# Forming two Strassen weight sums with a plain transfer and an adding transfer instead of a VectorE addition

## The chip, the cores and the metric

The kernel runs on one core of one Trainium2 chip. The metric is the device time of one execution in microseconds; lower is better. Engines are named as in the profile: PE is TensorE, DVE is VectorE, ACT is ScalarE, POOL is GpSimd and SP is SyncE. SP computes nothing here and issues all transfers of the kernel before. POOL does a few small operations.

## The reference

One decoder block in float32 on 512 tokens of width 1024: a half feed-forward layer with layer norm, a mixer (retention beside a convolution) with layer norm, and a second half feed-forward layer with layer norm.

```
def swiglu_ffn(h, w_gate, w_up, w_down):
    return (jax.nn.silu(h @ w_gate) * (h @ w_up)) @ w_down

x = layer_norm(alpha * x + 0.5 * swiglu_ffn(x, ffn1_w_gate, ffn1_w_up, ffn1_w_down), ln1_g, ln1_b)
m = hybrid_mixer(x, w_in, ...)
x = layer_norm(alpha * x + m, ln2_g, ln2_b)
x = layer_norm(alpha * x + 0.5 * swiglu_ffn(x, ffn2_w_gate, ffn2_w_up, ffn2_w_down), ln3_g, ln3_b)
```

The width of the feed-forward layers is 2816, which is 22 blocks of 128 columns. The change touches only the products with `w_gate` and `w_up`.

## The kernel before

**Precision.** Each float32 operand is split into a high part, which ACT makes by rounding to fp32r, and a low part, which DVE makes by subtracting the high part. Each product is three matmuls: high by high, high by low, low by high.

**Strassen units.** A feed-forward layer loads one unit of 128 x 2048 numbers (1 MB) for each of the 22 column blocks: gate and up weights together. The first units are done in the ordinary way (2 in the first layer, 3 in the second), the other 20 and 19, 39 in all, by a seven-product form of Strassen's method (Winograd's). For it the unit counts as four blocks of 128 x 512, in memory in the order a22, a12, a11, a21 (`raw[:, 0]` to `raw[:, 3]`). The weights that the products need are a12 and a11 as they are; s1 = a22 + a21 and s3 = a11 + a21; s2 = s1 + a11 and s4 = s2 + a12; and a22 as it is.

**Steps of one unit** (`strassen_w`, from line 144). `load` (L161) brings the unit into `raw`, on SP. `s13` (L165) forms s1 and s3 in one DVE addition into a tile `st`. `s24` (L169, L170) forms s2 and s4 from them and `raw`, in another `st` tile. `hi_a`, `hi_b`, `hi_c`, `hi_d` are the high parts on ACT (L155): of `raw` for a12 and a11, of the first `st` for s1 and s3, of the second `st` for s2 and s4 (named `chi`), of `raw` for a22 (`dhi`). `lo_a` to `lo_d` are the low parts on DVE (L158).

**Order.** The code around it is under a manual schedule: each engine does its instructions in the order in which they are written. In turn u of the loop in `strassen_rows` (from line 183), TensorE multiplies unit u (all at L201, 84 matmuls), while ACT and DVE prepare unit u + 1. A turn ends on DVE with `row2` (L226), which takes differences of PSUM banks; the second of them, `row2(prev, 1)`, stands at the head of the next turn and must be done before TensorE adds the s4 product into the same bank. Before the loop, the first unit is prepared among the steps that form the x operands (`f1` to `f4` at L125 and L127, `th` and `tl` at L135 and L138). These use the `st` tiles too.

**Buffers.** `raw` has two buffers, so the load of unit u + 2 waits for `lo_d` of unit u. `st` has three, taken in turn. In the first layer the order is f3, f1, s13 of the first unit, f2, s24 of the first unit, f4, s13 of the second unit: the last takes the buffer of f2 and so waits for f4, which reads f2. In the second layer s13 of the second unit takes the buffer of f1, whose last reader is `lo1` (the second of the two L138 instructions in a row).

Of the kernel before, what the change touches and what calls it, by code (L numbers as in the profile page):

```python
# [8 lines left out]
F32 = mybir.dt.float32  # L9
F32R = mybir.dt.float32r  # L10
AF = mybir.ActivationFunctionType
ALU = mybir.AluOpType
# [3 lines left out]
P = 128  # L16
# [36 lines left out]
def block_kernel(ctx, tc, ap, out):  # L53
    nc = tc.nc
# [92 lines left out]
    def strassen_w(pool, src):  # L147

        raw = wpool.tile([P, 4, 512], F32, name="raw", tag="raw", bufs=2)
        w, s = {}, {}  # L150

        def parts(n, shape, src, names, tag="w"):
            hi = (wpool if tag == "w" else pool).tile(shape, F32R, name=tag + "hi", tag=tag + "hi", bufs=n)
            lo = (wpool if tag == "w" else pool).tile(shape, F32R, name=tag + "lo", tag=tag + "lo", bufs=n)
            nc.scalar.copy(hi, src)  # L155
            for i, name in enumerate(names):
                w[name] = hi[:, i], lo[:, i]
            return lambda: nc.vector.tensor_tensor(lo, src, hi.bitcast(F32), op=ALU.subtract)  # L158

        def load():  # L160
            nc.sync.dma_start(raw, src.rearrange("p (b c) -> p b c", b=4))  # L161

        def s13():
            s[13] = pool.tile([P, 2, 512], F32, name="st", bufs=3)
            nc.vector.tensor_tensor(s[13], raw[:, 0:4:2], raw[:, 3:4].to_broadcast([P, 2, 512]), op=ALU.add)  # L165

        def s24():
            s[24] = pool.tile([P, 2, 512], F32, name="st", bufs=3)
            nc.vector.tensor_tensor(s[24][:, 0], s[13][:, 0], raw[:, 2], op=ALU.add)  # L169
            nc.vector.tensor_tensor(s[24][:, 1], s[24][:, 0], raw[:, 1], op=ALU.add)  # L170

        lo = {}

        def hi_a():
            lo["a"] = parts(4, [P, 2, 512], raw[:, 1:3], ("a12", "a11"))

        def hi_b():
            lo["b"] = parts(4, [P, 2, 512], s[13], ("s1", "s3"))

        def hi_c():  # L180
            lo["c"] = parts(2, [P, 2, 512], s[24], ("s2", "s4"), "c")

        def hi_d():
            lo["d"] = parts(2, [P, 1, 512], raw[:, 0:1], ("a22",), "d")

        return dict(w=w, load=load, s13=s13, s24=s24, hi_a=hi_a, hi_b=hi_b, hi_c=hi_c, hi_d=hi_d,
                    lo_a=lambda: lo["a"](), lo_b=lambda: lo["b"](), lo_c=lambda: lo["c"](), lo_d=lambda: lo["d"]())

# [450 lines left out]
    with ExitStack() as mix:  # L639
# [25 lines left out]
        with tc.tile_pool(name="heads", bufs=1) as hp_:  # L665
# [137 lines left out]
            for hp in range(H // 2):  # L803
                a, b = 2 * hp, 2 * hp + 1
# [199 lines left out]
```

## Time and profile before

| What | Value |
|---|---|
| Time, median of 3 runs (lowest, highest) | 1391.82 us (1391.26, 1392.65) |
| Time of the profiled execution | 1392.91 us |
| Its span, first to last instruction | 1391.1 us |
| Granted TensorE clock over the span | 0.996 |
| PE busy | 1373.3 us, 99% |
| DVE busy | 996.0 us, 72% |
| ACT busy | 597.5 us, 43% |
| POOL busy | 21.8 us, 2% |
| Transfers | 150.83 MB, 108 GB/s over the span |

The span is the time between the first and the last instruction on the core. The 1.8 us by which the profiled execution is longer lie around it. A share in the table is an average over stages: the Strassen stages run from about 30 to 238 us and from about 1067 to 1263 us of the span.

### The profile page before, as it was taken

How to read it: one execution, taken by the hardware profiler on the slowest of the kernel's cores; microseconds unless marked ns; L12 is line 12 of the kernel's file. 1: busy time of each engine (PE TensorE's matmuls, PEld its weight loads, DVE VectorE, ACT ScalarE, POOL GpSimd, SP SyncE). 2: the span in 40 equal slices, each digit the busy share in tenths (PEclk: the TensorE clock that was granted, in tenths of full speed). 3: DMA queues.
4: the chain of work that ended last, by engine and by line, in shares of the span. 5: the costliest groups of instructions: out<-in, count | busy, mean ns of one | idle time of the engine just before them, and what ended most of it. 6: DMA issues, size and time to landing. Idle time of an engine off the chain costs nothing.

```text
span 1391.1 us, 19272 instructions
## 1 busy us (share of the span) xinstructions
PE 1373.3 (99%) x7974; PEld 1218.3 (88%) x7974; DVE 996.0 (72%) x1422; ACT 597.5 (43%) x872; POOL 21.8 (2%) x36
## 2 busy tenths in 40 slices
PE   9899999999999999999999999999999999999997
PEld 7899999888988888888888888888889999998886
DVE  7888886434787787786787997555488887874336
ACT  5555555323434433434345522382333554544221
POOL 0000000000000000000000000000000000000000
PEclk9999999999999999999999999999999999999999
DMA  5323232524422222222221233232250323225221
GB/s 187 122 91 122 92 119 96 210 92 148 155 76 72 89 106 98 86 107 74 91 98 61 93 111 136 84 121 91 94 206 35 122 92 114 100 98 205 93 89 61
DMA packets 26006, 150.83 MB, mean 108 GB/s; under 512 B 2880, under 2 KB 3008, under 8 KB 10432
## 3 DMA queue, kind: packets, MB, share of 16 engines
q1 hardware_dynamic: 25920, 149.62, 29.9%
q8 instruction: 62, 1.02, 0.3%
q14 instruction: 24, 0.20, 0.0%
HBM read 143.32 MB, written 6.29 MB: 108 GB/s over the span
## 4 chain that ended last, share of the span: by engine, by line
PE 94%; DVE 4%; DMA 1%; ACT 0%; issue 0%; SPq 0%; POOL 0%; DVEq 0%; ACTq 0%
PE ps L201 27%; PE ps L435 19%; PE ps L293 13%; PE ps L294 13%; PE ps L292 13%; PE ps L707 2%; PE ps L708 2%; PE ps L709 2%; DMA h<-in_xT_dram 1%; PE ps L795 1%; DVE wlo L158 0%; DVE ln_y L404 0%; PE ps L416 0%; DVE tl L138 0%; DVE st L127 0%
## 5 line engine op out<-in xcount | busy, mean ns | idle before, releaser
L65 ACT CAST whi<-raw 128x1024 fp32r<-128x1024 f32 x156 | 162.4, 1051 | 270.7 <-PE ps L293 159.3
L66 DVE TENSOR_TENSOR wlo<-raw,whi 128x1024 fp32r<-128x1024 f32 x156 | 190.0, 1222 | 75.0 <-ACT whi L65 74.3
L292 PE MATMUL ps<-xh,whi 128*128 128x512 f32 x512 | 200.1, 391 | 0.0
L294 PE MATMUL ps<-xh,wlo 128*128 128x512 f32 x512 | 199.4, 389 | 0.5 <-DVE wlo L66 0.5
L293 PE MATMUL ps<-xl,whi 128*128 128x512 f32 x512 | 199.4, 389 | 0.0
L326 DVE SCALAR_TENSOR_TENSOR cv<-up,vec,cv 128x512 f32<-128x512 f32 x240 | 179.6, 748 | 4.2
L294 PEld LDWEIGHTS ps<-xh,wlo 128*128 128x128 f32 x512 | 96.1, 188 | 20.9 <-DVE wlo L66 1.0
L292 PEld LDWEIGHTS ps<-xh,whi 128*128 128x128 f32 x512 | 96.2, 188 | 19.5 <-ACT whi L65 0.2
L293 PEld LDWEIGHTS ps<-xl,whi 128*128 128x128 f32 x512 | 96.2, 188 | 19.3
L435 PE MATMUL ps<-whi,hh 128*128 128x512 f32 x320 | 100.0, 390 | 0.0
L435 PE MATMUL ps<-whi,hl 128*128 128x512 f32 x320 | 99.8, 389 | 0.0
L435 PE MATMUL ps<-wlo,hh 128*128 128x512 f32 x320 | 99.8, 389 | 0.0
L66 DVE TENSOR_TENSOR hl<-h,hh 128x512 fp32r<-128x512 f32 x40 | 27.3, 690 | 96.7 <-ACT hh L65 96.7
L201 PE MATMUL ps<-xh,whi 128*128 128x256 f32 x312 | 88.4, 283 | 0.0
L201 PE MATMUL ps<-xl,whi 128*128 128x256 f32 x312 | 88.3, 283 | 0.0
L201 PE MATMUL ps<-th,whi 128*128 128x256 f32 x312 | 88.3, 283 | 0.0
L201 PE MATMUL ps<-tl,whi 128*128 128x256 f32 x312 | 88.3, 283 | 0.0
L201 PE MATMUL ps<-xh,wlo 128*128 128x256 f32 x312 | 88.3, 283 | 0.0
L201 PE MATMUL ps<-th,wlo 128*128 128x256 f32 x312 | 88.3, 283 | 0.0
L209 ACT COPY z<-ps 128x256 f32<-128x256 f32 x78 | 29.1, 373 | 109.3 <-PE ps L201 109.0
L65 ACT CAST hh<-h 128x512 fp32r<-128x512 f32 x40 | 24.1, 623 | 115.1 <-PE ps L435 115.1
L435 PEld LDWEIGHTS ps<-wlo,hh 128*128 128x128 f32 x320 | 60.1, 188 | 12.5
(218 smaller groups left out, 3364.4 us busy)
## 6 DMA issues: line engine op xcount, KB each, us to landing
raw<-in_w_in_dram SPq DMA_DIRECT2D x40, 1024.0 KB, 4.8
raw<-in_w2gu_dram SPq DMA_DIRECT2D x22, 1024.0 KB, 4.8
raw<-in_w1gu_dram SPq DMA_DIRECT2D x21, 1024.0 KB, 4.8
raw<-in_w1dn_dram SPq DMA_DIRECT2D x11, 1024.0 KB, 4.9
raw<-in_w2dn_dram SPq DMA_DIRECT2D x11, 1024.0 KB, 4.8
raw<-in_w_ret_dram SPq DMA_DIRECT2D x8, 1024.0 KB, 4.8
ln_r<-scratch SPq DMA_DIRECT2D x8, 512.0 KB, 6.5
raw<-in_w_conv_dram SPq DMA_DIRECT2D x4, 1024.0 KB, 4.8
```

The costliest lines, as they stand in the source:

```text
L65: nc.scalar.copy(hi, src)
L66: nc.vector.tensor_tensor(lo, src, hi.bitcast(F32), op=ALU.subtract)
L201: mm(ps, a[:, sl], c[:, k, :], start=(first and k == 0 and n == 0), stop=(k == KH - 1 and n == 2), skip_group_check=True)
L209: nc.scalar.copy(t, ps)
L292: mm(ps, wh[wsl], xh[xsl], start=first, stop=False)
L293: mm(ps, wh[wsl], xl[xsl], start=False, stop=False)
L294: mm(ps, wl[wsl], xh[xsl], start=False, stop=last)
L326: op = nc.vector.scalar_tensor_tensor(c, up[:, t:t + S], vcol(C_CK + i * TAPS + t), c, op0=ALU.mult, op1=ALU.add)
L435: mm(acc[st][hf], x[:, sl], wx[:, hf * 512:(hf + 1) * 512], start=(k == 0 and x is ah and wi == 0), stop=(k == nk - 1 and x is al),)
L707: mm(o, xh[:, k, ssl], wh[:, csl], start=(k == 0), stop=False)
L708: mm(o, xh[:, k, ssl], wl[:, csl], start=False, stop=False)
L709: mm(o, xl[:, k, ssl], wh[:, csl], start=False, stop=(k == KD - 1))
```

## The change

In `load` SP now issues a second, plain transfer behind the one into `raw`: the blocks a22 and a11 go from device memory into the tile for s1 and s3. POOL then issues a transfer that reads a21 twice and adds it onto both blocks. The tile is taken in `load`, and `s13` does nothing; `s24`, `hi_b` and `lo_b` read the tile as before. Each of the 39 units gets 1 MB more of transfers, in two of 512 KB.

```diff
         def load():
-            nc.sync.dma_start(raw, src.rearrange("p (b c) -> p b c", b=4))
+            blocks = src.rearrange("p (b c) -> p b c", b=4)
+            nc.sync.dma_start(raw, blocks)
+
+            s[13] = pool.tile([P, 2, 512], F32, name="st", bufs=3)
+            nc.sync.dma_start(s[13], blocks[:, 0:4:2])
+            nc.gpsimd.dma_start(s[13], blocks[:, 3:4].to_broadcast([P, 2, 512]), accum_op=ALU.add)
 
         def s13():
-            s[13] = pool.tile([P, 2, 512], F32, name="st", bufs=3)
-            nc.vector.tensor_tensor(s[13], raw[:, 0:4:2], raw[:, 3:4].to_broadcast([P, 2, 512]), op=ALU.add)
+            pass
```

The order of the instructions, first on DVE in the first turn of the loop in the first layer, where the second unit is prepared (before). What stands in brackets are the semaphores waited for: DMAHW of a transfer of SP, DMASW of a transfer of POOL, the others of an engine.

```order
L521 TENSOR_TENSOR h<-ps,sg 128x512 [waits Activation_49]
L165 TENSOR_TENSOR st<-raw 128x1024 [waits DMAHW7_49]
L158 TENSOR_TENSOR wlo<-raw,whi 128x1024 [waits Activation_49]
L158 TENSOR_TENSOR wlo<-st,whi 128x1024 [waits Activation_49]
L521 TENSOR_TENSOR h<-ps,sg 128x512 [waits Activation_49]
L169 TENSOR_TENSOR st<-st,raw 128x512
L170 TENSOR_TENSOR st<-st,raw 128x512 [waits DVE_49]
L226 TENSOR_TENSOR up_347<-ps,z_421 128x256 [waits PE_49]
L158 TENSOR_TENSOR clo<-st,chi 128x1024 [waits Activation_49]
L158 TENSOR_TENSOR dlo<-raw,dhi 128x512 [waits Activation_49]
L226 TENSOR_TENSOR up_347<-y_401,ps 128x256 [waits PE_49]
```

The same place after the change (lines from L163 on are four higher than before, so L173 and L174 are `s24`, L230 is `row2` and L525 was L521):

```order
L525 TENSOR_TENSOR h<-ps,sg 128x512 [waits Activation_49]
L158 TENSOR_TENSOR wlo<-raw,whi 128x1024 [waits DMAHW0_49,Activation_49]
L158 TENSOR_TENSOR wlo<-st,whi 128x1024 [waits DMASW1_49,Activation_49]
L525 TENSOR_TENSOR h<-ps,sg 128x512 [waits Activation_49]
L173 TENSOR_TENSOR st<-st,raw 128x512
L174 TENSOR_TENSOR st<-st,raw 128x512 [waits DVE_49]
L230 TENSOR_TENSOR up_351<-ps,z_423 128x256 [waits PE_49]
L158 TENSOR_TENSOR clo<-st,chi 128x1024 [waits Activation_49]
L158 TENSOR_TENSOR dlo<-raw,dhi 128x512 [waits Activation_49]
L230 TENSOR_TENSOR up_351<-y_405,ps 128x256 [waits PE_49]
```

The addition is gone, nothing else has changed places, and the low part of s1 and s3 now waits for POOL's transfer (as does the high part on ACT).

On SP at the start of the kernel, the loads of the first Strassen units, before:

```order
L75 DMA raw<-in_w1gu_dram 128x2048 [waits DMAHW5_49]
L161 DMA raw<-in_w1gu_dram 128x2048 [waits DMAHW6_49,DMAHW0_49,DVE_49]
L161 DMA raw<-in_w1gu_dram 128x2048 [waits DMAHW7_49,DMAHW5_49,DVE_49]
L161 DMA raw<-in_w1gu_dram 128x2048 [waits DMAHW6_49,DVE_49]
L161 DMA raw<-in_w1gu_dram 128x2048 [waits DMAHW7_49,DMAHW1_49,DVE_49]
```

And after:

```order
L75 DMA raw<-in_w1gu_dram 128x2048 [waits DMAHW5_49]
L162 DMA raw<-in_w1gu_dram 128x2048 [waits DMAHW6_49,DMAHW0_49,DVE_49]
L165 DMA st<-in_w1gu_dram 128x2x512 [waits DMAHW7_49]
L162 DMA raw<-in_w1gu_dram 128x2048 [waits DMAHW5_49,DVE_49]
L165 DMA st<-in_w1gu_dram 128x2x512 [waits DMAHW1_49,DVE_49]
L162 DMA raw<-in_w1gu_dram 128x2048 [waits DMAHW6_49,DMAHW2_49,DVE_49]
L165 DMA st<-in_w1gu_dram 128x2x512 [waits DMAHW3_49,DMASW0_49]
```

Each load is followed by the plain transfer into `st`; that of the second unit waits for DVE (for f4). On POOL there is one adding transfer for each unit, in the order of the units, each waiting for the plain transfer of its own unit; in the second layer the plain transfer of the first unit stands on SP behind the stores of the layer norm before it.

## Rows read from the trace of the kernel before

**Rows 1.** Busy time of each engine, from the page.
```profile
PE 1373.3 (99%) x7974; PEld 1218.3 (88%) x7974; DVE 996.0 (72%) x1422; ACT 597.5 (43%) x872; POOL 21.8 (2%) x36
```

**Rows 2.** Instruction groups, costliest first: line, engine, operation, count, busy us, mean ns.
```profile
L165 DVE TENSOR_TENSOR st<-raw 128x1024 f32<-128x1024 f32 x39 | 47.5, 1219 | 0.0
```

**Rows 3.** Waits of PE: waiting and releasing line, us, times, longest.
```profile
PE ps L201 <- DVE up L226: 5.5, 2, 3.2
...
PE ps L201 <- ACT y L209: 0.9, 1, 0.9
```

**Rows 4.** Windows: length, busy time of each engine, granted clock, DMA share, GB/s.
```profile
47.00:51.00 4.00, 4.00 (x23) 4.00 (x22) 3.97 (x5) 2.57 (x4) 0.00 (x0) 0.58 0.69 262
...
1082.00:1086.00 4.00, 4.00 (x23) 4.00 (x23) 3.96 (x6) 2.75 (x4) 0.00 (x0) 0.59 0.77 262
...
60.00:230.00 170.00, 170.00 (x1419) 170.00 (x1418) 137.22 (x183) 87.31 (x151) 0.00 (x0) 1.00 0.30 106
```

**Rows 5.** Timeline of DVE, first layer: start us, length, instruction, [idle before].
```profile
26.96 0.69 DVE L169 TENSOR_TENSOR st<-st,raw 128x512 f32<-128x512 f32 x1
...
31.71 1.42 DVE L127 TENSOR_TENSOR st<-st,h 128x256 f32<-128x256 f32 x4
...
37.59 1.22 DVE L165 TENSOR_TENSOR st<-raw 128x1024 f32<-128x1024 f32 x1
...
39.98 1.23 DVE L158 TENSOR_TENSOR wlo<-st,whi 128x1024 fp32r<-128x1024 f32 x1
```

**Rows 6.** Timeline of ACT, first layer.
```profile
19.98 1.05 ACT L155 CAST whi<-raw 128x1024 fp32r<-128x1024 f32 x1 [0.51 <-DMA raw<-in_w1gu_dram]
...
38.05 0.38 ACT L209 COPY z<-ps 128x256 f32<-128x256 f32 x1
38.89 1.05 ACT L155 CAST whi<-st 128x1024 fp32r<-128x1024 f32 x1 [0.47 <-DVE st L165]
```

**Rows 7.** Timeline of PE, first layer: the matmul behind the longest wait.
```profile
46.46 0.39 PE L201 MATMUL ps<-xh,chi 128*128 128x256 f32 x1 [3.19 <-DVE up L226]
```

**Rows 8.** Timeline of SP: loads of the first and third Strassen unit.
```profile
13.89 0.33 SPq L161 DMA_DIRECT2D raw<-in_w1gu_dram  x1
...
36.10 0.33 SPq L161 DMA_DIRECT2D raw<-in_w1gu_dram  x1
```

**Rows 9.** Transfers: issuing queue, count, KB each, median us from issue to landing.
```profile
raw<-in_w1gu_dram SPq DMA_DIRECT2D x21, 1024.0 KB, 4.8
...
ln_r<-scratch SPq DMA_DIRECT2D x8, 512.0 KB, 6.5
...
ln_g<-in_ln_dram SPq DMA_DIRECT2D x3, 512.0 KB, 3.7
```

**Rows 10.** Landing times of the transfers into raw that start before 60 us.
```profile
DMA to landing us min/median/max: 3.5/5.5/8.5
```

**Rows 11.** Timeline of SP, second layer: the last stores of the layer norm.
```profile
1040.74 0.99 SPq L406 DMA_DIRECT2D scratch<-ln_y  x2
```

**Rows 12.** Timeline of DVE, second layer.
```profile
1050.55 0.69 DVE L169 TENSOR_TENSOR st<-st,raw 128x512 f32<-128x512 f32 x1
...
1061.40 2.36 DVE L138 TENSOR_TENSOR tl<-st,th 128x1024 fp32r<-128x1024 f32 x2
...
1070.43 0.42 DVE L238 TENSOR_TENSOR g<-z,ps 128x256 f32<-128x256 f32 x1 [4.28 <-PE ps L201]
```

**Rows 13.** Timeline of ACT, second layer: high parts for the second unit.
```profile
1073.24 0.37 ACT L209 COPY z<-ps 128x256 f32<-128x256 f32 x1
1073.76 1.05 ACT L155 CAST whi<-st 128x1024 fp32r<-128x1024 f32 x1
```

**Rows 14.** Timeline of SP: load of the fifth unit of the second layer.
```profile
1088.70 0.33 SPq L161 DMA_DIRECT2D raw<-in_w2gu_dram  x1
```

**Rows 15.** Timeline of ACT: high part of s1 and s3 of that unit.
```profile
1102.15 1.05 ACT L155 CAST whi<-st 128x1024 fp32r<-128x1024 f32 x1
```

**Rows 16.** Timeline of DVE: s2 and the last low part of that unit.
```profile
1103.00 0.68 DVE L169 TENSOR_TENSOR st<-st,raw 128x512 f32<-128x512 f32 x1
...
1107.93 0.69 DVE L158 TENSOR_TENSOR dlo<-raw,dhi 128x512 fp32r<-128x512 f32 x1
```

## The prediction

> **What bounds the kernel now.** I read the busy times first: PE 1373.3 of 1391.1 us, DVE 996.0 [rows 1]. Then, for the stage that the change touches, a table by window: from 60 to 230 us PE is busy for all of 170.00 us, DVE for 137.22 [rows 4]. There DVE is late for nobody. The addition that goes costs 39 x 1219 ns = 47.5 us of DVE [rows 2]; in the steady part of both Strassen stages all of that is time in which nobody waits for DVE. So I looked for the places where PE does wait for DVE: two waits on `row2`, 5.5 us together, the longest 3.2 [rows 3]. They stand in the first turn of each stage, where the second unit is prepared: PE stops until 46.46 in the first layer [rows 7]; the other 2.3 us are in the second layer. Half a microsecond to a microsecond after each wait ends, PE's granted clock is down: 0.58 and 0.59 over 4 us [rows 4], that is 1.2 GHz for most of them, some (1 - 0.58) x 4 = 1.7 us lost each time. All that the change can win or lose, unless it breaks the steady part, is at these two places.
>
> **The change part by part.** Call X the time from POOL's issue of the adding transfer to its landing. No row shows a transfer issued by POOL, nor one that adds. From below: 512 KB alone land after 3.7 us [rows 9]. From above: a load at the crowded start took 8.5 us [rows 10]. The adding transfer reads 512 KB of weights and the 512 KB of the tile it adds onto, which is a full unit's 1024 KB (4.8 us alone [rows 9]), and in the first layer it runs beside loads of units: that of the third unit is issued at 36.10 [rows 8]. The nearest row is a transfer of 512 KB beside others, 6.5 us [rows 9]; I take X = 6.0. For 512 KB plain and alone I take 3.7, and 0.1 us for a queue to see a landing.
>
> First layer, first unit. `raw` has landed when ACT starts on it, at 19.98 [rows 6]. The plain transfer stands right behind it; 512 KB more cost 4.8 - 3.7 = 1.1 us [rows 9], so it lands at 21.1, and the sum at 21.1 + 0.1 + 6.0 = 27.2. Before, `s24` began at 26.96 [rows 5]. DVE would now be there some 0.9 us sooner (one addition less, but `hi_a` holds `lo_a` until 21.03), and waits: +0.2 us against before. DVE is without a break from there to f4, which ended at 31.71 + 1.42 = 33.13 [rows 5] and now ends at 33.35.
>
> First layer, second unit. Its plain transfer waits for f4 (buffer of f2), so it is issued at 33.35, lands at 37.05, and the sum lands at 37.05 + 0.1 + 6.0 = 43.15. Before, `hi_b` began at 38.89, held by the addition [rows 6]; with the sum there it could begin when the copy ends, 38.43, so at best the change wins 0.5 us. By my X it loses 43.15 - 38.89 = 4.3 us. Behind `hi_b` on ACT and `lo_b` on DVE stand `s24`, `hi_c`, `lo_c`, `lo_d` and then `row2`, for which PE waits; that is a chain of 7.6 us (38.89 to 46.46 [rows 6, 7]) without slack. PE resumes at 50.8 instead of 46.46. The 0.9 us that PE waits for ACT's y copy [rows 3] lie ahead of this wait and are swallowed by it.
>
> Second layer, first unit. SP comes to the plain transfer after the last stores, 1041.73 [rows 11]: it lands at 1045.4, the sum at 1051.5, against `s24` at 1050.55 [rows 12]: +0.95 us. DVE works on without a break to `lo1`, which ended at 1061.40 + 2.36 = 1063.76 [rows 12], now 1064.7. Nothing of this reaches PE by itself: DVE has 4.28 us to spare before 1070.43 [rows 12].
>
> Second layer, second unit. Its plain transfer waits for `lo1`: issued at 1064.7, landed at 1068.4, sum at 1074.5. `hi_b` began at 1073.76 [rows 13], and could begin at 1073.61 at best. So +0.75 us, with the same chain to PE behind it.
>
> Steady part. The load of the fifth unit is issued at 1088.70 [rows 14], the plain transfer at its heels; with 4.8 + 1.1 us both are there by 1094.95, the sum by 1101.05. ACT wants it at 1102.15 [rows 15], and DVE, one addition earlier than before, at 1101.8 [rows 16]. So nothing waits, and by the traffic there is room: a DMA share of 0.30 at one unit of 1 MB a turn [rows 4] becomes about 0.6 with twice the bytes, 0.75 if the adding one counts double. What keeps it stable: from `s24` to the end of `lo_d`, which frees `raw`, 1108.62 - 1103.00 = 5.6 us [rows 16]; 0.35 + 4.8 + 1.1 + 0.1 + X + 5.6 must fit into two turns of 10.08 us (84 matmuls at 120 ns): X up to 8.2 us costs nothing.
>
> The clock. It falls after each long wait of PE; a wait of 7.5 us instead of 3.2 could leave a longer stretch at 1.2 GHz or let part of it fall into the idle time. The trace has only waits of 3.2 and 2.4 us, both followed by 1.7 us of loss; I leave it as it is and put 1.7 us to either side.
>
> Sum: 4.3 + 0.75 = +5.05 us. On the profiled execution (1392.91 us, span 1391.1) that is 1398.0. It lies 1.1 us above the median of the runs, 1391.82, so the median to expect is 1396.9.
>
> A rule that bears on X: the Trainium skill's "DMA: Bandwidth & Descriptors" (Anatomy of one DMA — SWDGE (gpsimd) path) puts a transfer from POOL at 2.0 us plus the bytes over 436 GB/s, 3.2 us for 512 KB. Its "Collectives: The Full Stack" (The bandwidth ceiling) says that an add needs two source reads for each write and so runs at half the rate, which makes 4.4 us by the same figures. The rows for plain transfers (3.7 and 4.8 us) are a little above that first formula (3.2 and 4.4); no run here shows the second rule. By 4.4 us the sum would be that of the first rival below.
>
> **The rivals.**
>
> *The transfers are hidden.* X is about 5 or less. With X = 3.7 the first sum is there at 24.9, `s24` begins at 26.05, f4 ends at 32.2, the second sum lands at 39.7, and PE resumes 0.8 us later than before; the second layer wins 0.15. With X = 4.4: +1.4 in all. With X = 5: `s24` at 26.2, the second sum at 41.2, +2.3, and 0.15 won in the second layer: +2.1 us. So 1392.5 to 1393.9, not slower by what can be told. The mechanism is that transfer time hides behind f2 to f4, and it decides at X = 5.35, where the sum is 2.8. For it: 3.7 and 4.8 us alone. Against it: each adding transfer of the first layer runs beside a load of 1 MB, and POOL's issue comes on top.
>
> *The steady part breaks.* X above 8.2 us. At X = 10 two turns take 21.95 instead of 20.16 us: 0.9 us a unit, 36 units, +32 us; at the two starts X = 10 costs 12.3 us (first layer) and 8.7 (second). That is +53 in all: about 1445. For it: nothing here shows how fast an adding transfer is. Against it: the crowded start, 8.5 us, is the worst among the transfers into `raw`, and the steady part has much less traffic.
>
> *The clock stays up.* If the adding transfers are quicker than a plain one alone (X of 2.5), the waits of PE shrink by 0.5 and 0.15 us, and if the shorter waits no longer bring the clock down, 1.7 us come back each: -4.0 us, 1387.8. Against it: even a wait of 2.4 us brought it down, and no transfer of 512 KB here is that quick.
>
> **How the numbers follow.** A measurement of this kernel can tell about 0.2%, 2.8 us, from no change. The forecast (X from 5.35 to 8.2 us; +2.8 to +14) has 0.56; hidden 0.26; the steady part breaks 0.13; the clock stays up 0.05. Slower is 0.56 + 0.13 = 0.69, within 0.2% 0.26, faster 0.05. The sum moves by some 4 us for each us of X (the wait counts twice at each start, through the first unit and through the second), so the range is wide: from X = 4 (+1, 1392.8), less 1 us for a part of the clock's loss, to X = 8 (+13) with the clock's 1.7 above it, 1406.5; I go on to 1410 for the first of the breaking cases.
>
> **What would show it.** In the profile after: L165's 47.5 us of DVE are gone, 39 transfers issued by POOL appear, whose landing time gives X directly. Right is the forecast if ACT's `hi_b` of the second unit waits for a transfer of POOL and starts near 43, PE's wait on `row2` in the first layer is near 7.5 us and in the second near 3, and from 60 to 230 us PE is still busy throughout. PE waits inside that window would mean that the steady part breaks; `hi_b` at 38.4 to 41 that the transfers are hidden. What would make it wrong beside X: another wait ahead of POOL's issue, or a plain transfer that lands much later than 3.7 us after its issue.

## The result, and the profile after

The changed kernel takes 1455.71 us (median of 4 runs, 1449.85 to 1458.9), the kernel before 1391.54 in the runs beside it: 1.0456 times as long (95% interval 1.0439 to 1.0473), +64 us. The prediction said 1396.9 and slower, the range ended at 1410. The direction was right, the size was not: what came is the rival to which it gave 0.13, the steady part that breaks.

Busy time of each engine after, from the page, for [rows 1]:

```profile
PE 1399.3 (96%) x7974; PEld 1240.4 (85%) x7974; DVE 953.0 (65%) x1383; ACT 594.4 (41%) x872; POOL 69.0 (5%) x75
```

DVE has lost its 39 additions. PE has done the same 7974 matmuls in 26.0 us more, and the span has grown by 66.0 (1457.1 against 1391.1), so some 40 us are idle time of PE and 26 are matmuls that took longer at a lower clock (0.976 granted over the span, 0.996 before). The waits of PE, for [rows 3] (waiting and releasing line, us, times, longest):

```profile
PE ps L205 <- ACT y L213: 31.9, 13, 3.9
PE ps L205 <- ACT whi L155: 8.6, 2, 5.2
PE ps L205 <- DVE up L230: 5.7, 2, 3.0
```

The waits on `row2` are as long as before. New are twelve of the 13 waits on the y copy (one before [rows 3]): that copy stands on ACT behind `hi_b`, which waits for POOL's transfer. In the window from 60 to 230 us (busy time of each engine, granted clock, DMA share, GB/s), for the third of [rows 4], and in one stretch of 4 us behind such a wait:

```profile
60.00:230.00 170.00, 156.49 (x1224) 155.47 (x1223) 104.00 (x146) 75.12 (x131) 18.05 (x15) 0.93 0.66 179
...
75.00:79.00 4.00, 3.85 (x19) 3.85 (x20) 4.00 (x7) 2.64 (x7) 0.69 (x1) 0.57 0.64 102
```

PE is no longer busy throughout, and after a wait its clock is at 1.2 GHz for most of the next 4 us, as after the two waits of before. The mean DMA share of 0.66 suggests that the 16 engines could carry more; the first experiment tests that. Their landing times, for [rows 9] (count, KB each, median us from issue to landing):

```profile
raw<-in_w1gu_dram SPq DMA_DIRECT2D x21, 1024.0 KB, 6.4
...
st<-in_w1gu_dram SPq DMA_DIRECT2D x20, 512.0 KB, 8.3
st<-in_w1gu_dram POOLq DMA_DIRECT2D x20, 512.0 KB, 7.3
```

The plain transfer into `st` takes 8.3 us, the adding one 7.3. The chain that ended last, from 60 to 130 us (start us, length, what):

```profile
79.53 7.25 DMA st<-in_w1gu_dram
...
86.84 0.50 issue
87.34 10.98 DMA st<-in_w1gu_dram
...
99.30 0.38 ACT y L213
...
99.72 11.61 PE ps L205 x84
...
112.82 8.32 DMA st<-in_w1gu_dram
...
121.71 7.34 DMA st<-in_w1gu_dram
```

Read it as a cycle. SP issues the plain transfer of a unit at 79.53; it lands 7.25 us later; 0.6 us on, POOL's adding transfer starts and takes 10.98; then ACT's copy follows, for which PE waited. The loads of `raw` on SP show the same pace:

```profile
79.11 0.33 SPq L162 DMA_DIRECT2D raw<-in_w1gu_dram  x1
...
88.07 0.33 SPq L162 DMA_DIRECT2D raw<-in_w1gu_dram  x1
...
103.67 0.33 SPq L162 DMA_DIRECT2D raw<-in_w1gu_dram  x1
...
112.40 0.33 SPq L162 DMA_DIRECT2D raw<-in_w1gu_dram  x1
```

Every second load is one chain: two interleaved chains of some 24.4 us here (24.56 and 24.33), where two turns of PE are 20.16. This stretch is a slow one. Over the whole window PE did 1224 matmuls in 170 us, which makes 23.3 us for two turns of 84. Transfers, not PE, set the pace.

The chain at the start, first layer:

```profile
13.74 7.92 DMA st<-in_w1gu_dram
...
21.98 7.25 DMA st<-in_w1gu_dram
...
38.70 9.90 DMA st<-in_w1gu_dram
...
48.68 1.05 ACT whi L155
...
56.23 3.78 PE ps L205 x16
```

`hi_b` of the second unit starts at 48.68 (38.89 before [rows 6]) and PE resumes at 56.23 (46.46 [rows 7]): 9.8 us. How much the first layer lost in all is read from POOL's first operation of the second layer norm, ahead of the second layer, in before and then after:

```profile
1018.37 0.56 POOL L402 TENSOR_TENSOR ln_i<-ln_v,mhalf 128x1 f32<-128x1 f32 x1 [126.44 <-DVE ln_v L397]
```

```profile
1053.00 0.56 POOL L406 TENSOR_TENSOR ln_i<-ln_v,mhalf 128x1 f32<-128x1 f32 x1 [126.42 <-DVE ln_v L401]
```

That is 34.6 us. PE's resumption in the second layer, before and then after, is 8.1 us later than this shift alone:

```profile
1081.33 0.39 PE L201 MATMUL ps<-xh,chi 128*128 128x256 f32 x1 [2.36 <-DVE up L226]
```

```profile
1124.02 0.58 PE L205 MATMUL ps<-xh,chi 128*128 128x256 f32 x1 [2.69 <-DVE up L230]
```

So:

| Where | Lost, us | How worked out |
|---|---|---|
| First layer, start | 9.8 | 56.23 - 46.46 |
| First layer, steady part | 24.9 | 34.6 - 9.8 |
| Second layer, start | 8.1 | 1124.02 - 1081.33 - 34.6 |
| Second layer, steady part | 23.3 | 66.0 - 34.6 - 8.1 |

### The profile page after: what moved, and what is told of

It reads as the page before. It is cut to its first block, busy times and chain, and to the rows that moved or that the text cites. A ratio compares the mean times of both kernels' runs of the same rounds, so it can differ in the third digit from the quotient of the medians.

```text
span 1457.1 us, 19473 instructions
## 1 busy us (share of the span) xinstructions
PE 1399.3 (96%) x7974; PEld 1240.4 (85%) x7974; DVE 953.0 (65%) x1383; ACT 594.4 (41%) x872; POOL 69.0 (5%) x75
## 3 DMA queue, kind: packets, MB, share of 16 engines
q0 software_dynamic: 10608, 20.45, 8.8%
## 4 chain that ended last, share of the span: by engine, by line
PE 71%; DMA 18%; DVE 7%; issue 2%; ACT 1%; SPq 0%; POOL 0%; DVEq 0%; POOLq 0%; ACTq 0%
PE ps L439 18%; PE ps L297 12%; PE ps L298 12%; PE ps L296 12%; DMA st<-in_w1gu_dram 9%; PE ps L205 9%; DMA st<-in_w2gu_dram 8%; PE ps L711 2%; PE ps L713 2%; PE ps L712 2%; DVE clo L158 1%; DVE st L173 1%; DVE st L174 1%; DVE h L581 1%; DVE dlo L158 1%
## 5 line engine op out<-in xcount | busy, mean ns | idle before, releaser
L296 PEld LDWEIGHTS ps<-xh,whi 128*128 128x128 f32 x512 | 96.2, 188 | 19.5
L205 PE MATMUL ps<-th,whi 128*128 128x256 f32 x312 | 94.1, 302 | 8.6 <-ACT whi L155 8.6
L173 DVE TENSOR_TENSOR st<-st,raw 128x512 f32<-128x512 f32 x39 | 26.9, 689 | 105.3 <-DMA st<-in_w1gu_dram 54.1
L205 PE MATMUL ps<-th,wlo 128*128 128x256 f32 x312 | 93.0, 298 | 1.2 <-DVE wlo L158 1.2
L205 PE MATMUL ps<-tl,whi 128*128 128x256 f32 x312 | 93.0, 298 | 0.0
L155 ACT CAST whi<-st 128x1024 fp32r<-128x1024 f32 x39 | 40.9, 1049 | 116.3 <-DMA st<-in_w1gu_dram 58.7
L205 PE MATMUL ps<-th,dhi 128*128 128x256 f32 x156 | 49.3, 316 | 31.9 <-ACT y L213 31.9
```

The source lines that it names most:

```text
L205: mm(ps, a[:, sl], c[:, k, :], start=(first and k == 0 and n == 0), stop=(k == KH - 1 and n == 2), skip_group_check=True)
L296: mm(ps, wh[wsl], xh[xsl], start=first, stop=False)
```

## The experiments

The theory (A): the loss is one of latency. In the steady part, the chain from the freeing of a buffer to its next freeing has to fit into two turns, and does not; at the starts the same transfers are waited for once. Against it stand: the traffic itself is too much (B), and the addition is what is slow (C) or POOL's issue (D).

**The plain transfer first.**

```diff
-            nc.sync.dma_start(raw, blocks)
             s[13] = pool.tile([P, 2, 512], F32, name="st", bufs=3)
             nc.sync.dma_start(s[13], blocks[:, 0:4:2])
             nc.gpsimd.dma_start(s[13], ..., accum_op=ALU.add)
+            nc.sync.dma_start(raw, blocks)
```

> The same transfers, only the plain one into st is issued ahead of the load of raw. Theory A (latency: in the steady part the chain from the freeing of a buffer by way of the plain transfer, the adding transfer, s24 and the low parts to the next freeing is longer than two turns, 24.4 us against 20.16): the plain transfer no longer runs behind 1 MB (some 4.5 us instead of 8.3), and st is free before raw is (lo_c instead of lo_d, 1.4 us earlier), so the chain falls to 19 to 21 us and most of the 48 us lost in the steady part come back: 1405 to 1425 us. Theory B (the 16 DMA engines cannot carry the traffic of a unit in a turn): the traffic is the same, 1445 us or more.

1411.27 us (ratio to before 1.0139, 1.0124 to 1.0155): 44 us of the 64 are back with not a byte less moved. The window from 60 to 230 us, and the two transfers:

```profile
60.00:230.00 170.00, 170.00 (x1419) 170.00 (x1419) 124.72 (x169) 89.31 (x153) 19.25 (x16) 1.00 0.79 208
```

```profile
st<-in_w1gu_dram SPq DMA_DIRECT2D x20, 512.0 KB, 4.7
st<-in_w1gu_dram POOLq DMA_DIRECT2D x20, 512.0 KB, 6.6
```

PE is busy for all of the window at full clock, and the DMA share is higher (0.79) than in the changed kernel. B falls: the engines carry this traffic at full pace. The plain transfer lands in 4.7 us instead of 8.3. It is also issued before the load instead of behind it, and need not wait for `raw` to come free; the run does not separate the two effects. What is left, 19.5 us, lies at the starts. PE resumes there, first and then second layer, at:

```profile
53.65 0.58 PE L204 MATMUL ps<-xh,chi 128*128 128x256 f32 x1 [2.70 <-DVE up L229]
```

```profile
1099.34 0.58 PE L204 MATMUL ps<-xh,chi 128*128 128x256 f32 x1 [2.69 <-DVE up L229]
```

That is 7.2 us lost in the first layer. In the second it is 11.0 (1099.34 - 1081.33 - 7.0, the shift ahead of that layer), more than the 8.1 of the changed kernel: there the adding transfer runs beside the loads of the second and the third unit and takes 11.7 us. The order cures the steady part, not the starts.

**POOL's transfer without the addition.**

```diff
-            nc.gpsimd.dma_start(s[13], blocks[:, 3:4].to_broadcast([P, 2, 512]), accum_op=ALU.add)
+            nc.gpsimd.dma_start(s[13], blocks[:, 3:4].to_broadcast([P, 2, 512]))
```

> POOL's transfer without the addition: it overwrites the tile, so s1 and s3 are both a21. Same bytes read from memory, same waits, same issue by POOL. Theory C (the addition itself is slow in the DMA engines): POOL's transfer lands in about 5 us instead of 7.3 alone and 10 beside others, two turns fit in 21 to 22 us, the starts lose 9 instead of 18: 1405 to 1425 us. Theory D (POOL's issue and the queueing behind other transfers make the length, adding is free): within 8 us of 1455.

1418.24 us (1.0193, 1.0176 to 1.021). So 37 of the 64 us go with the addition. That is inside C's range; D, by which adding is free, falls. Read from the profile as in the table above, the two starts lose 4.6 and 4.7 us instead of 9.8 and 8.1, and the steady part 13.6 instead of 48.2. The landing times of POOL's 39 transfers, from the start of POOL's instruction, without the addition and then with it:

```profile
DMA to landing us min/median/max: 4.9/6.6/8.5
```

```profile
DMA to landing us min/median/max: 5.8/7.2/11.0
```

Adding makes the shortest 0.9 us longer, the median 0.6 and the longest 2.5. The issue was expected to be the same and was not: POOL is busy with it for 0.72 us instead of 1.20, and these times hold that half microsecond too. The 26 us that stay lost without the addition belong to the rest of the chain: POOL's issue, the plain transfer (8.0 us), and what runs beside.

**The first two units of each layer on DVE.**

```diff
         def load():
             ...
             nc.sync.dma_start(raw, blocks)
+            if by_dve:
+                return
...
         def s13():
-            pass
+            if not by_dve:
+                return
+            s[13] = pool.tile([P, 2, 512], F32, name="st", bufs=3)
+            nc.vector.tensor_tensor(s[13], raw[:, 0:4:2], ..., op=ALU.add)
```

> The first two units of each layer get s1 and s3 from DVE as before, the other 35 by transfers. If the 17.8 us (9.8 and 8.1) lost at the starts and the 48 us lost later are separate losses, as Theory A has it: 1391.5 + 44 to 48 = 1435 to 1441 us, PE resumes at 46.5 in the first layer as before. If the steady loss is the start's lateness that is handed on from turn to turn: about 1392 to 1400.

1444.8 us (1.038, 1.0365 to 1.0396). PE resumes in the first layer as before, and yet 53 us are lost: the steady part makes its loss by itself and does not inherit it.

```profile
46.17 0.39 PE L210 MATMUL ps<-xh,chi 128*128 128x256 f32 x1 [3.18 <-DVE up L235]
```

The time is 4 us above the upper end expected; with an early start the 35 units lose 1.5 us each, where the 37 or so of the changed kernel lost 1.3.

**Three blocks in raw.** Nothing reads a21 from `raw` any more.

```diff
-            nc.sync.dma_start(raw, blocks)
+            nc.sync.dma_start(raw[:, 0:3], blocks[:, 0:3])
```

> raw gets three of its four blocks (a21 is read from raw by nothing any more): 768 KB a unit instead of 1 MB, same waits. Theory A with contention: the plain transfer lands 0.6 to 1 us earlier and the adding one, which runs beside the load of the next unit, about 0.6 to 1 us earlier, 1.2 to 2 us off the 24.4 of two turns: 0.6 to 1 us a unit, 23 to 38 us: 1418 to 1434 us. If only the fixed times of the transfers count and not what runs beside them: 1450 or more.

1431.28 us (1.0287, 1.0271 to 1.0303): 24 us less for 256 KB less a unit, as expected for transfers that lengthen each other (medians in the first layer 7.7 and 6.8 us instead of 8.3 and 7.3).

**Both cures together:** the plain transfer first, and the starts on DVE.

> Both cures together: the plain transfer ahead of the load of raw, and the first two units of each layer on DVE. If the loss consists of the starts and of a chain longer than two turns, and of nothing else, nothing is left: 1391 to 1393 us, PE waits as in the kernel before (5.5 and 0.9 us). If the extra traffic costs something of its own (35 units with 1 MB more each), some microseconds remain: 1395 us or more.

1391.71 us (0.9996, 0.9987 to 1.0005). PE's waits, and the window:

```profile
PE ps L210 <- DVE up L235: 5.5, 2, 3.2
...
PE ps L210 <- ACT y L218: 0.9, 1, 0.9
```

```profile
60.00:230.00 170.00, 170.00 (x1419) 170.00 (x1419) 124.42 (x169) 88.70 (x153) 19.25 (x16) 1.00 0.75 204
```

To within some 2 us, as the interval has it, all 64 are accounted for: chain and starts, and nothing else. It also shows what the change was worth at best: DVE has 35 additions less (in the window 124.42 us instead of 137.22) and the time is that of the kernel before.

**The same with three blocks** in `raw`.

> e5 with three blocks in raw for the 35 units (768 KB instead of 1 MB). If e5 has lost nothing, there is nothing to win: within 1.5 us of e5. If e5 still loses to traffic, this is faster than e5 by part of that.

1391.82 us (0.9997, 0.9988 to 1.0006): nothing left to win by less traffic.

**Every second unit.** Order as changed, transfers for units 3, 5, 7 and so on alone (`by_dve` as above; the first unit is on DVE too).

```diff
-            n = strassen_w(pool, units[u + 1]) if not last else None
+            n = strassen_w(pool, units[u + 1], u % 2 == 0) if not last else None
```

> Order of the changed kernel (load of raw first), but transfers for every second unit only, from the third unit on; the others and the first two by DVE. If the chain is too long because each adding transfer runs beside the next unit's three transfers, it now has a neighbour of 1 MB alone: 0.4 + 5.9 + 0.6 + 7 to 8 + 5.6 = 19.5 to 20.5 us against two turns of 20.16: 1391 to 1400 us. If each transferred unit costs its share of the 53 us that were lost with all 35 of them: 1391.5 + 26 = 1418 us.

1392.35 us (1.0007, 0.9998 to 1.0016). Half the transfers cost nothing measurable, where a share would have been 26 us: a chain that fits is free, one that does not costs every turn. Here it fits narrowly, with 1.7 us of PE's time gone in this window:

```profile
60.00:230.00 170.00, 168.34 (x1399) 167.87 (x1399) 127.16 (x174) 85.20 (x148) 9.63 (x8) 1.00 0.52 152
```

**The addition on POOL instead**, from `raw` as before the change, with no transfers.

```diff
-            nc.vector.tensor_tensor(s[13], raw[:, 0:4:2], raw[:, 3:4].to_broadcast([P, 2, 512]), op=ALU.add)
+            nc.gpsimd.tensor_tensor(s[13], raw[:, 0:4:2], raw[:, 3:4].to_broadcast([P, 2, 512]), op=ALU.add)
```

> No extra transfers: POOL instead of DVE does the addition for s1 and s3, from raw, as soon as raw has landed. The price of the addition on POOL is in no trace of this case. If it takes up to some 5 us, hi_b of the second unit is held by nothing and begins 0.5 us sooner in the first layer and 0.15 in the second, and DVE's 47.5 us are gone for nothing: 1390.5 to 1391.5, not to be told from before. If it takes 10 us or more, or holds up DVE's reads, the starts lose as with the transfers: 1395 us or more.

1401.02 us (1.0063, 1.005 to 1.0075): +9, though the addition takes 2.6 us in the mean and the steady part loses nothing. POOL's group, then DVE's f4 beside one of these additions (32.25 to 34.77 us), then PE:

```profile
L165 POOL TENSOR_TENSOR st<-raw 128x1024 f32<-128x1024 f32 x39 | 99.5, 2552 | 320.7 <-DMA raw<-in_w1gu_dram 134.0 <-DMA raw<-in_w2gu_dram 131.2 <-DVE wlo L158 23.1
```

```profile
32.09 3.63 DVE L127 TENSOR_TENSOR st<-st,h 128x256 f32<-128x256 f32 x4
```

```profile
39.85 0.58 PE L201 MATMUL ps<-th,dhi 128*128 128x256 f32 x1 [4.30 <-ACT y L209]
```

f4 took 1.42 us before [rows 5] and takes 3.63 while POOL reads: DVE is 2.2 us longer beside an addition of 2.52. At the starts, where DVE is what PE waits for, that is a loss: PE resumes at 50.68 in the first layer instead of 46.46. In the steady part DVE has the time (PE is busy for all of the 170 us). The 0.5 us hoped for drowned in it. No version ran faster than the kernel before.

## Why the prediction was wrong

**What bounds.** Right: DVE's 47.5 us are hidden. With nothing else in the way, taking 35 of the 39 additions from DVE moved the time by nothing that can be measured.

**The steady part: the step that failed.** "So nothing waits" rested on 4.8 + 1.1 us until the plain transfer is there and X = 6.0 behind it, and on a limit of X up to 8.2. Measured, the plain transfer took 8.3 us from its own issue, so that it was there 0.4 + 8.3 = 8.7 us after the issue of the load instead of 0.35 + 4.8 + 1.1 = 6.25; and X was 0.6 + 7.3 = 7.9, beside other transfers up to 0.6 + 11.0. With 8.3 us for the plain one, two turns leave X some 20.16 - (0.4 + 8.3 + 5.2) = 6.3 (5.2 for `s24` to `lo_d`, as from 98.42 to 103.64), and no X was as short as that: the shortest of the 39 was 0.6 + 5.8. Neither error alone breaks the sum. With the measured plain transfer and the forecast X (0.1 + 6.0) two turns need 20.0 of 20.16 us, with the forecast plain transfer and X = 7.9 some 19.4. The terms were taken from transfers that ran alone or once; in the steady part each plain transfer runs behind 1 MB and beside the adding transfer of the unit ahead. That the three together fit in the engines' time was checked (0.6 to 0.75 of it, measured 0.66 to 0.79) and is a different question from whether the chain fits in two turns.

**X.** 6.0 was low. Its bounds, 3.7 and 8.5, held the median and not the crowded ones (9.8 to 11.0). The engines are full while an adding transfer runs alone. Here is one microsecond of that in the changed kernel, and one with plain loads (last two columns DMA share and GB/s):

```profile
77.00:78.00 1.00, 1.00 (x7) 1.00 (x7) 1.00 (x2) 0.15 (x1) 0.00 (x0) 0.50 0.98 166
82.00:83.00 1.00, 1.00 (x11) 1.00 (x10) 0.99 (x2) 0.89 (x2) 0.00 (x0) 1.00 1.00 418
```

At a full share of the 16 engines that is 166 GB/s against 418. The two differ in more than the addition, however. POOL's transfer without it, alone in the run that left it out, does little better:

```profile
69.00:70.00 1.00, 1.00 (x11) 1.00 (x10) 1.00 (x2) 0.52 (x1) 0.00 (x0) 1.00 0.78 188
70.00:71.00 1.00, 1.00 (x11) 1.00 (x10) 1.00 (x3) 0.12 (x1) 0.00 (x0) 1.00 0.70 143
```

The rows for POOL's queue on the two pages of the profile (packets, MB, share of the 16 engines' span) allow a price for each of the 39 transfers, first with the addition (span 1457.1 us), then without (1414.0):

```profile
q0 software_dynamic: 10608, 20.45, 8.8%
```

```profile
q0 software_dynamic: 5616, 20.45, 6.8%
```

That is 3.3 us of all 16 engines with the addition and 2.5 without it: a third more, and not twice as much. The Trainium skill's "Collectives: The Full Stack" (The bandwidth ceiling) says that an add reads two sources and so halves the rate. These totals do not show the half. The addition also changes the number of packets, so the runs do not isolate the rule. Why POOL's transfer without the addition is so much slower than a plain load is open.

**The starts.** Forecast +4.3 and +0.75, measured +9.8 and +8.1. The mechanism was right in both (`hi_b` of the second unit waits for POOL's transfer, with the whole chain to `row2` behind it); X was 7.6 and 10.4 in the first layer and 7.5 and 10.3 in the second, and counts twice at each start, as said.

**A buffer.** The sections on the kernel before and on the change, and the prediction, say that the second unit's `st` in the first layer takes the buffer of f2 and waits for f4. The times say otherwise. SP issued its plain transfer at 34.18, just after `lo_c` of the first unit ended (34.15), while f4 ended at 35.49; so it took the buffer of the first unit's s2 and s4. A pool that gives out the buffer freed first, and not the next in turn, would do that, but no run tests it. The slip made the forecast of this start some 1.3 us too late, against the other errors.

**The clock.** It was left at two losses of 1.7 us, 1.7 to either side. There were 17 waits of PE of this kind instead of three, and TensorE's busy time grew by 26.0 us for the same matmuls. How much of these 26 lies on the chain is open: the chain from 99.72 to 111.33 has 11.6 us of matmuls that take 10.08 at full clock, but most of the rest of that stretch runs through transfers.

**The rivals.** The one that came was named and had its condition in the wrong place. It asked for X above 8.2; the median X of 7.9 was enough, because the plain transfer took 2.45 us more. The prediction had such a transfer among its signs of being wrong, but not in the sum. That the price, +53 with X = 10, came near the measured +64 is partly luck: it put 32 us into the steady part and 21 into the starts, where 48 and 18 were measured.

## What to carry to other kernels

An operation that is off the critical path buys nothing when it is taken away, and what replaces it can be on the path: here a chain of two transfers per unit in place of 1.2 us on an engine that had time to spare. For a chain that recurs, add up every link under the traffic that the change itself makes, and hold the sum against the time that the buffers allow (two buffers, two turns); a mean share of the engines below 1 says nothing about it. If it does not fit, the order of issue is the first thing to change: the transfer that others wait for goes ahead of the one that has time (44 of 64 us here).

## What the runs showed of the hardware

- A transfer of POOL that adds 512 KB onto a tile holds the 16 DMA engines for some 3.3 us, the same transfer without the addition for 2.5 (worked out from the shares of POOL's queue). Alone at a full share the adding one moved 166 GB/s, plain loads 418. It is made of 272 packets (10608 for 39), without the addition of 144 (5616 for 39).
- POOL is busy for 1.20 us with issuing an adding transfer of 512 KB and 0.72 us with a plain one, and starts 0.5 us after the awaited landing.
- Transfers on SP's and POOL's queues lengthen each other: the same plain 512 KB land in 4.0 us (issued at 34.18, nothing beside), 4.7 (first in line) or 10.1 (behind 1 MB and beside an adding one).
- DVE's additions of two tiles hardly advance while POOL adds two tiles: 1.42 us became 3.63 beside an addition of 2.52. The Trainium skill's "SBUF — State Buffer" (Who interferes with whom) says that a DVE instruction with two SBUF inputs contends with one of GpSimd that reads SBUF; the trace agrees, and DVE is the one that waits here.
